# Weighting the early expert dot products while their gates are built, and prefetching the other gates

## The chip, the cores and the metric

One core of one Trainium2 chip runs the kernel. The metric is device time in microseconds (us) for one execution; the time before is the median of three runs. Engines are called PE (TensorE), DVE (VectorE), ACT (ScalarE), POOL (GpSimd) and SP (SyncE, which here only issues DMAs).

## The reference

The model is a decoder block on 512 tokens of width 1024. Two token mixers (a gated linear attention and a sparse latent attention) feed a residual stream; then a product-key expert layer (PEER) is applied, and this last layer is what the change touches:

```python
u = expert_u[ix]                       # ix: for each token, 8 heads x 16 experts of 16384
v = expert_v[ix]
a = gelu(einsum('td,thkd->thk', hx, u)) * gx     # gx: softmax weight of each picked expert
out = einsum('thk,thkd->td', a, v)
```

All arithmetic is float32.

## The kernel before, in words

The 512 tokens are two halves of 256. For the first half the expert layer is done by gathering: each picked expert's rows are fetched by an indirect DMA (POOL, L998), multiplied with the token on DVE (L1003) and added up on DVE (L1012). This `gather()` is a generator that runs in the background: `pump()` moves it on by a fixed share of a step wherever the other code calls it. `behind(i)` marks a DVE instruction after which the next gather instructions are to be issued.

For the second half (NDT = 256 tokens) the layer is done densely over all 16384 experts, in 128 chunks `ib` of 128 experts:

- `dots_of(ib)` loads two chunks of u (tile `up`, 1 MB, every second call), multiplies one chunk with the 256 tokens (`projT`, L184, one PSUM bank `pmm` of two) and writes Gelu of the result with ACT (L936) into a tile `a` of 128 x 256. Forty-eight such tiles (AHEAD = 48) can be held.
- `build_g(Tt)` builds the gate of every expert for every token, which is zero nearly everywhere. For 16 tokens at a time (a gate tile `gs` of 128 x 128 x 16, two buffers; 16 such tiles, eight for each of the token tiles Tt = 2 and 3), in two blocks of 8 tokens: DVE makes two comparison masks `pm` (L884) and `eq` (L887), ACT scales one into `qm` (L893), PE multiplies them (L898, in PSUM banks `psc` and `ptr`), ACT copies the result into `gs` (L899). Then ACT copies the gates of chunks 0 to 7 into two tiles `first_g` (L903), and SP writes the others, chunks 8 to 127, to a DRAM tensor `gd` (L904, 960 KB).
- `dense()` goes over the chunks: `weigh(ib + 5)` multiplies a dot product tile by its gate on DVE (L956); the gate of chunks from 8 on comes from `gd` in tiles `gtile` of eight chunks (L952, 1 MB, one buffer, asked for when the first of the eight is weighed). The weighted tile and the v chunk are each split into a high and a low part (L116 on ACT, L117 on DVE), and twelve matmuls (L186 to L188) add to four PSUM banks. Then one more dot product may be made, so that 80 of the 128 are made inside `dense()`.

Around it: dot products 0 to 7 are made before the experts of token tile 2 are picked, 8 to 23 before those of tile 3 are picked; `build_g(2)` is stepped between the parts of that second pick, and `build_g(3)` between dot products 24 to 47, one step (8 tokens) after each. Text order is a priority: a scheduler at compile time gives each engine a fixed order, in which an instruction goes ahead of earlier text if it is ready sooner by the scheduler's reckoning. On the chip each engine, and SP's queue of DMAs, then keeps its order. The tiles of `dense()` (pool `dn`) take over the memory of the tiles of `build_g` (pool `gb`), and each waits until the tile that lay there is free.

Of the kernel before, what the change touches and what calls it, by code (L numbers as in the profile page):

```python
# [59 lines left out]
def hybrid_block_kernel(ctx, tc, x, c_col, w_ada, b_ada, b_col, g1_col, g2_col, wT, wN, wM, w_br, w_o,  # L60
# [33 lines left out]
        nc.gpsimd.tensor_tensor(dst, dst, mhalf[:, :w], op=ALU.pow)  # L94

    x2d = [dr.tile([P, D], F32, name=f"x2d{i}") for i in range(NT)]
    gd = dr.tile([P // 8, P, NDT // GB, 8, GB], F32, name="gd")
    kvd = [dr.tile([2, P, TH], F32, name=f"kvd{i}") for i in range(8)]
    gated = [dr.tile([P, D], F32, name=f"gated{i}") for i in range(2)]

# [775 lines left out]
    def build_g(Tt):  # L876

        TB = 8
        for tb in range((Tt - NG) * P // GB, (Tt - NG + 1) * P // GB):
            gs = gb.tile([P, P, GB], F32, name="gs", bufs=2)  # L880
            for b in range(0, GB, TB):
                t0 = tb * GB + b
                pm = gb.tile([P, TB, P], F32, name="pm", bufs=2)
                nc.vector.tensor_tensor(pm, iof[:, None, :].to_broadcast([P, TB, P]),  # L884
                                        i2T[:, t0:t0 + TB, None].to_broadcast([P, TB, P]), op=ALU.is_equal)
                e = gb.tile([P, TB // 2, P, 2], BF16, name="eq", bufs=2)
                pace[0] = nc.vector.tensor_tensor(  # L887
                    e, iob[:, None].to_broadcast([P, TB // 2, P, 2]),
                    i1T[:, t0:t0 + TB].rearrange("p (g t) -> p g t", t=2)[:, :, None, :].to_broadcast([P, TB // 2, P, 2]),
                    op=ALU.is_equal).ins  # L890
                qm = gb.tile([P, TB, P], F32, name="qm", bufs=2)
                for t in range(TB):
                    nc.scalar.activation(qm[:, t], e[:, t // 2, :, t % 2], AF.Copy, scale=gaT[:, t0 + t:t0 + t + 1])  # L893
                for t4_ in range(0, TB, 4):
                    turn[0] += 1
                    p = (psc, ptr)[turn[0] % 2]().rearrange("p (t i) -> p t i", t=4)
                    for t in range(4):
                        nc.tensor.matmul(p[:, t], pm[:, t4_ + t], qm[:, t4_ + t], start=True, stop=True)  # L898
                    nc.scalar.copy(gs[:, :, b + t4_:b + t4_ + 4], p.rearrange("p t i -> p i t"))  # L899
                pump()  # L900
                yield
            for q in range(2):
                nc.scalar.copy(first_g[q][:, tb], gs[:, 4 * q:4 * q + 4])  # L903
            nc.sync.dma_start(gd.rearrange("c p b i t -> b p c i t")[tb, :, 1:], gs.rearrange("p (c i) t -> p c i t", i=8)[:, 1:])  # L904


    def finish(Tt, x2, peer):
# [18 lines left out]
    def dots_of(ib):  # L926
# [5 lines left out]
            nc.sync.dma_start(up[0], u_t[ib // 2])  # L932
        p = pmm(True)
        projT(p[:, :NDT], [up[0][:, ib % 2]], h2[1])
        a = ap.tile([P, NDT], F32, name="a", bufs=AHEAD)
        nc.scalar.activation(a, p[:, :NDT], AF.Gelu)  # L936
        return a

    def dense(ahead):
        banks = [psc, psc, ptr, ptr]  # L940
        acc = [[banks[2 * i + n]() for n in range(2)] for i in range(NT - NG)]
        gt = [None]
        weighted = []

        def weigh(ib):

            if ib < 8:
                g = first_g[ib // 4][:, :, ib % 4]
            else:
                if ib % 8 == 0:  # L950
                    gt[0] = dn.tile([P, NDT // GB, 8, GB], F32, name="gtile", bufs=1)
                    nc.sync.dma_start(gt[0], gd[ib // 8])  # L952
                g = gt[0][:, :, ib % 8]
            a = ahead.pop(0)
            a3 = a.rearrange("p (b t) -> p b t", t=GB)
            behind(nc.vector.tensor_tensor(a3, a3, g, op=ALU.mult))  # L956
            weighted.append(a)

        made = [len(ahead)]
        for ib in range(LEAD):  # L960
            weigh(ib)
        late_ops = []
        vb = x2 = None
        for ib in range(P):
# [6 lines left out]
                    nc.sync.dma_start(x2[:, i], x2d[NG + i])  # L971
            if ib + LEAD < P:
                weigh(ib + LEAD)
            a = hp.tile([P, 2, NDT], F32R, name="as", tag="h" + "hl"[ib % 2])
            v = wp.tile([P, 2, D], F32R, name="vs", tag="w2", bufs=2)
            split(a[:, 0], a[:, 1], weighted.pop(0))
            split(v[:, 0], v[:, 1], vb[:, ib % 2])
            a, v = [[t[:, 0], t[:, 1]] for t in (a, v)]
            late_ops.append((ib, a, v))
# [8 lines left out]
                        mm(acc[i][n], [t[:, ts_] for t in a], [t[:, ns] for t in v], jb == 0, jb == P - 1)  # L988
            late_ops.clear()
            while made[0] < AHEAD + (ib + 1) * (P - AHEAD) // (P - 16) and made[0] < P:  # L990
                ahead.append(dots_of(made[0]))
                made[0] += 1
            pump()
        for i in range(NT - NG):
            finish(NG + i, x2[:, i], acc[i])
# [133 lines left out]
    nc.gpsimd.iota(iob, pattern=[[1, P], [0, 2]], base=0, channel_multiplier=0, allow_small_or_imprecise_dtypes=True)  # L1129
    iof = gb.tile([P, P], BF16, name="iof")  # L1130
    nc.gpsimd.iota(iof, pattern=[[1, P]], base=0, channel_multiplier=0, allow_small_or_imprecise_dtypes=True)
    ahead = []

    first_g = [wp.tile([P, NDT // GB, 4, GB], F32, name="first_g", tag="raw", bufs=NRAW) for _ in range(2)]
    building = iter(())
    background[:] = [[gat, RATE_G, 0.0]]
    for Tt in range(NG, NT):
        ahead += [dots_of(len(ahead) + i) for i in range(DOTS[Tt - NG])]
        for h0 in range(0, 8, HG):
            for _ in pick(Tt, h0):  # L1140
                next(building, None)
# [2 lines left out]
        picks_T(Tt)  # L1144
        drain(building)
        building = build_g(Tt)
    while len(ahead) < AHEAD:
        ahead.append(dots_of(len(ahead)))
        next(building, None)
    drain(building)  # L1150
    rest_eng.close()
# [2 lines left out]
    nc.sync.dma_start(fing, rowb(fin_g, D))  # L1154
    nc.sync.dma_start(gate2, gated[1])
    background[:] = [[gat, RATE_DENSE, 0.0]]
    dense(ahead)
    drain(gat)


# [65 lines left out]
```

## Time and profile before

| what | value |
|---|---|
| median of three runs | 1875.56 us (1866.99 to 1878.46) |
| profiled execution, whole | 1862.8 us |
| its span (first to last instruction) | 1860.9 us |
| PE busy | 1723.5 us (93%) |
| DVE busy | 1431.9 us (77%) |
| ACT busy | 722.9 us (39%) |
| moved by DMA | 583.81 MB, mean 314 GB/s |

All views below are of the one profiled execution. "Busy" of PE is modelled from pipelined matmuls. The granted clock is a share of full speed: 1.00 is 2.4 GHz, and the lower of the two levels is 1.2 GHz. The gates are built from about 1005 to 1157 us, the dense stage runs from about 1180 to 1849 us.

### The profile page before, as it was taken

How to read it: one execution, taken by the hardware profiler on the slowest of the kernel's cores; microseconds unless marked ns; L12 is line 12 of the kernel's file. 1: busy time of each engine (PE TensorE's matmuls, PEld its weight loads, DVE VectorE, ACT ScalarE, POOL GpSimd, SP SyncE). 2: the span in 40 equal slices, each digit the busy share in tenths (PEclk: the TensorE clock that was granted, in tenths of full speed). 3: DMA queues.
4: the chain of work that ended last, by engine and by line, in shares of the span. 5: the costliest groups of instructions: out<-in, count | busy, mean ns of one | idle time of the engine just before them, and what ended most of it. 6: DMA issues, size and time to landing. Idle time of an engine off the chain costs nothing.

```text
span 1860.9 us, 24908 instructions
## 1 busy us (share of the span) xinstructions
PE 1723.5 (93%) x8898; PEld 1462.8 (79%) x8898; DVE 1431.9 (77%) x2993; ACT 722.9 (39%) x1693; POOL 504.7 (27%) x459
## 2 busy tenths in 40 slices
PE   6999999989999988989999889898999999999995
PEld 3888999878766876877778778687778888887874
DVE  5798545339999778658997888778778887887886
ACT  3544465333121134002245767333334433433443
POOL 0012000001563556643441555111112121211120
PEclk8999999989998999989999999899999999999998
DMA  8757566625886899996776999999989999999992
GB/s 292 287 182 265 192 193 206 225 88 204 285 294 215 313 338 385 392 378 243 279 284 238 393 369 359 415 422 394 401 345 410 392 404 393 412 410 372 421 361 99
DMA packets 156238, 583.81 MB, mean 314 GB/s; under 512 B 14529, under 2 KB 51521, under 8 KB 121426
## 3 DMA queue, kind: packets, MB, share of 16 engines
q1 hardware_dynamic: 100818, 313.76, 45.4%
q0 software_dynamic: 55296, 268.46, 37.4%
q8 instruction: 70, 1.15, 0.2%
q14 instruction: 54, 0.44, 0.1%
HBM read 559.10 MB, written 23.07 MB: 313 GB/s over the span
## 4 chain that ended last, share of the span: by engine, by line
PE 52%; DVE 17%; issue 12%; DMA 12%; POOL 5%; ACT 2%; SPq 0%; POOLq 0%; DVEq 0%; ACTq 0%
PE pmm L184 19%; DMA grow<-rows,ids 6%; POOL grow L998 4%; DVE grow L1003 3%; PE pmx L184 3%; PE pmm L188 2%; PE pmm L187 2%; PE pmm L186 2%; PE psc L187 2%; PE psc L188 2%; DMA gd<-gs 2%; PE ptr L188 2%; PE ptr L187 2%; DMA gtile<-gd 2%; PE psc L186 2%
## 5 line engine op out<-in xcount | busy, mean ns | idle before, releaser
L998 POOL DMA_INDIRECT grow<-rows,ids x384 | 446.9, 1164 | 897.9 <-DVE h2n L1012 500.6
L184 PE MATMUL pmm<-h2h,up 128*128 128x256 f32 x2048 | 470.2, 381 | 4.4 <-ACT a L936 2.8
L184 PEld LDWEIGHTS pmm<-h2h,up 128*128 128x128 f32 x2048 | 384.8, 191 | 57.4 <-ACT a L936 3.6
L1003 DVE SCALAR_TENSOR_TENSOR grow<-grow,h2n 128x1024 f32<-128x1024 f32 x256 | 310.0, 1217 | 56.0 <-DMA grow<-rows,ids 55.6
L1012 DVE SCALAR_TENSOR_TENSOR gacc<-grow,dots,gacc 128x1024 f32<-128x1024 f32 x127 | 162.2, 1277 | 18.9 <-DMA grow<-rows,ids 18.2
L117 DVE TENSOR_TENSOR vs<-vb,vs 128x1024 fp32r<-128x1024 f32 x128 | 158.1, 1235 | 22.8 <-ACT vs L116 22.7
L1012 DVE SCALAR_TENSOR_TENSOR h2n<-grow,dots,h2n 128x1024 f32<-128x1024 f32 x127 | 162.3, 1278 | 0.0
L116 ACT CAST vs<-vb 128x1024 fp32r<-128x1024 f32 x128 | 133.3, 1042 | 0.0
L117 DVE TENSOR_TENSOR w<-raw,w 128x1024 fp32r<-128x1024 f32 x79 | 98.0, 1240 | 45.7 <-ACT w L116 45.3
L187 PE MATMUL psc<-vs,as 128*128 128x512 f32 x256 | 104.5, 408 | 26.5 <-DVE vs L117 26.5
L186 PE MATMUL psc<-vs,as 128*128 128x512 f32 x256 | 115.8, 459 | 6.4 <-ACT vs L116 6.4
L116 ACT CAST w<-raw 128x1024 fp32r<-128x1024 f32 x79 | 82.6, 1046 | 72.7 <-PE pmm L188 33.1
L936 ACT ACTIVATE a<-pmm 128x256 f32<-128x256 f32 x128 | 49.0, 383 | 149.0 <-PE pmm L184 148.7
L188 PE MATMUL psc<-vs,as 128*128 128x512 f32 x256 | 102.6, 401 | 0.0
L184 PE MATMUL pmm<-hh,raw 128*128 128x256 f32 x416 | 98.5, 384 | 3.8 <-DVE yp L687 1.9
L188 PE MATMUL ptr<-vs,as 128*128 128x512 f32 x256 | 101.9, 398 | 0.0
L187 PE MATMUL ptr<-vs,as 128*128 128x512 f32 x256 | 101.8, 398 | 0.0
L186 PE MATMUL ptr<-vs,as 128*128 128x512 f32 x256 | 100.3, 397 | 0.0
L116 ACT CAST as<-a 128x256 fp32r<-128x256 f32 x128 | 51.5, 402 | 121.7 <-PE ptr L188 118.9
L1051 ACT ACTIVATE dots<-dots 128x1 f32<-128x1 f32 x128 | 25.9, 202 | 173.9 <-DVE grow L1003 173.6
L94 POOL TENSOR_TENSOR rs<-rs,mhalf 128x1 f32<-128x1 f32 (+1 forms) x24 | 18.1, 755 | 266.3 <-DVE rs L93 266.2
L184 PEld LDWEIGHTS pmm<-hh,raw 128*128 128x128 f32 x416 | 77.0, 191 | 16.2 <-DVE yp L687 2.3
(375 smaller groups left out, 3521.5 us busy)
## 6 DMA issues: line engine op xcount, KB each, us to landing
up<-u_t SPq DMA_DIRECT2D x64, 1024.0 KB, 9.4
vb<-v_t SPq DMA_DIRECT2D x64, 1024.0 KB, 9.3
raw<-wT SPq DMA_DIRECT2D x74, 512.0 KB, 4.5
adaw<-w_ada SPq DMA_DIRECT2D x20, 1024.0 KB, 6.8
raw<-wN SPq DMA_DIRECT2D x32, 512.0 KB, 4.3
raw<-w_br SPq DMA_DIRECT2D x32, 512.0 KB, 4.6
raw<-w_pq SPq DMA_DIRECT2D x32, 512.0 KB, 4.3
gd<-gs SPq DMA_DIRECT2D x16, 960.0 KB, 10.0
```

What stands on the lines that cost most here:

```text
L94: nc.gpsimd.tensor_tensor(dst, dst, mhalf[:, :w], op=ALU.pow)
L116: (hi_eng or nc.scalar.copy)(hi, src)
L117: i = (eng or nc.vector).tensor_tensor(lo, src, hi.bitcast(F32), op=ALU.subtract)
L184: nc.tensor.matmul(dst, a[0], b[0], start=first, stop=last, **kw)
L186: nc.tensor.matmul(dst, a[0], b[0], start=first, stop=False, **kw)
L187: nc.tensor.matmul(dst, a[0], b[1], start=False, stop=False, **kw)
L188: nc.tensor.matmul(dst, a[1], b[0], start=False, stop=last, **kw)
L936: nc.scalar.activation(a, p[:, :NDT], AF.Gelu)
L998: nc.gpsimd.indirect_dma_start(out=dst, out_offset=None, in_=table, in_offset=bass.IndirectOffsetOnAxis(ap=index[0][:, r:r + 1], axis=0))
L1003: nc.vector.scalar_tensor_tensor(u, u, 1.0, h2n[i], op0=ALU.mult, op1=ALU.mult, accum_out=dots[i][:, r:r + 1])
L1012: nc.vector.scalar_tensor_tensor(gacc, v, w, gacc, op0=ALU.mult, op1=ALU.add)
L1051: nc.scalar.activation(w, w, AF.Gelu)
```

## The change

Four things are done:

1. The 48 tiles `a` become one tile `kept` of 48 rows x 256 tokens. While a gate tile is built, the dot products made so far in the text (`m` of them: 24 for the first eight gate tiles, 27 to 41 for the others) are multiplied by their gates on DVE, in one instruction. For the chunks up to 47 whose dot products come later in the text, ACT copies the gates into their rows of `kept`.
2. A dot product of chunk 24 to 47 then finds `d` of its 256 tokens with a gate already in its row. For these ACT writes Gelu to a small tile `dg` (two buffers), and DVE multiplies it onto the row; for the other tokens ACT writes Gelu to the row as before.
3. Gates of chunks 0 to 47 are no longer written to `gd` or read back: a write is 640 KB, and ten gate tiles are read instead of fifteen. `first_g` is gone, and `weigh` does nothing below chunk 48.
4. The ten are read with two buffers: chunks 48 to 55 are asked for at the start of `dense()`, ahead of its first v chunk, and each next eight when the eight before them begin to be weighed. The second buffer lies where half of the `as` tiles were; `as` becomes one tile with four parts in the other half.

```diff
-    gd = dr.tile([P // 8, P, NDT // GB, 8, GB], F32, name="gd")
+    gd = dr.tile([(P - AHEAD) // 8, P, NDT // GB, 8, GB], F32, name="gd")
...
-            for q in range(2):
-                nc.scalar.copy(first_g[q][:, tb], gs[:, 4 * q:4 * q + 4])
-            nc.sync.dma_start(gd.rearrange("c p b i t -> b p c i t")[tb, :, 1:], gs.rearrange("p (c i) t -> p c i t", i=8)[:, 1:])
+            m, ts_ = made[0], slice(tb * GB, (tb + 1) * GB)
+            if m:
+                behind(nc.vector.tensor_tensor(kept[:, :m, ts_], kept[:, :m, ts_], gs[:, :m], op=ALU.mult))
+            if m < AHEAD:
+                nc.scalar.copy(kept[:, m:, ts_], gs[:, m:AHEAD])
+            built[0] = (tb + 1) * GB
+            nc.sync.dma_start(gd.rearrange("c p b i t -> b p c i t")[tb], gs.rearrange("p (c i) t -> p c i t", i=8)[:, AHEAD // 8:])
...
-        a = ap.tile([P, NDT], F32, name="a", bufs=AHEAD)
-        nc.scalar.activation(a, p[:, :NDT], AF.Gelu)
-        return a
-
-    def dense(ahead):
+        a = kept[:, ib % AHEAD]
+        d = built[0] if ib < AHEAD else 0
+        if d < NDT:
+            nc.scalar.activation(a[:, d:], p[:, d:NDT], AF.Gelu)
+        if d:
+            t = gb.tile([P, NDT], F32, name="dg", bufs=2)[:, :d]
+            nc.scalar.activation(t, p[:, :d], AF.Gelu)
+            behind(nc.vector.tensor_tensor(a[:, :d], a[:, :d], t, op=ALU.mult))
+        made[0] += 1
+
+    def dense():
...
+        as4 = hp.tile([P, 4, 2, NDT], F32R, name="as", tag="hh")
+        gts = []
+
+        def load_g(c):
+
+            if c < P // 8:
+                pool, tag = ((dn, "gtile"), (hp, "hl"))[c % 2]
+                gts.append(pool.tile([P, NDT // GB, 8, GB], F32, name="gtile", tag=tag))
+                nc.sync.dma_start(gts[-1], gd[c - AHEAD // 8])
+
+        load_g(AHEAD // 8)
 
         def weigh(ib):
 
-            if ib < 8:
-                g = first_g[ib // 4][:, :, ib % 4]
-            else:
-                if ib % 8 == 0:
-                    gt[0] = dn.tile([P, NDT // GB, 8, GB], F32, name="gtile", bufs=1)
-                    nc.sync.dma_start(gt[0], gd[ib // 8])
-                g = gt[0][:, :, ib % 8]
-            a = ahead.pop(0)
-            a3 = a.rearrange("p (b t) -> p b t", t=GB)
-            behind(nc.vector.tensor_tensor(a3, a3, g, op=ALU.mult))
-            weighted.append(a)
-
-        made = [len(ahead)]
-        for ib in range(LEAD):
-            weigh(ib)
+            if ib < AHEAD:
+                return
+            if ib % 8 == 0:
+                load_g(ib // 8 + 1)
+            a3 = kept[:, ib % AHEAD].rearrange("p (b t) -> p b t", t=GB)
+            behind(nc.vector.tensor_tensor(a3, a3, gts[ib // 8 - AHEAD // 8][:, :, ib % 8], op=ALU.mult))
+
...
-            a = hp.tile([P, 2, NDT], F32R, name="as", tag="h" + "hl"[ib % 2])
+            a = as4[:, ib % 4]
             v = wp.tile([P, 2, D], F32R, name="vs", tag="w2", bufs=2)
-            split(a[:, 0], a[:, 1], weighted.pop(0))
+            split(a[:, 0], a[:, 1], kept[:, ib % AHEAD])
...
+    kept = ap.tile([P, AHEAD, NDT], F32, name="kept")
+    made, built = [0], [0]
```

## Rows read from the trace of the kernel before

**Rows 1.** The page: engine, busy us, share of the span, instructions.
```profile
PE 1723.5 (93%) x8898; PEld 1462.8 (79%) x8898; DVE 1431.9 (77%) x2993; ACT 722.9 (39%) x1693; POOL 504.7 (27%) x459
...
DMA packets 156238, 583.81 MB, mean 314 GB/s; under 512 B 14529, under 2 KB 51521, under 8 KB 121426
```
**Rows 2.** Stretches: length, busy of PE, PEld, DVE, ACT, POOL, clock, DMA.
```profile
1005.00:1073.00 68.00, 62.53 (x393) 56.93 (x392) 56.35 (x53) 55.02 (x169) 35.05 (x25) 0.95 0.98 347
1073.00:1157.00 84.00, 74.06 (x435) 67.31 (x434) 68.48 (x66) 61.30 (x189) 45.87 (x33) 0.94 1.02 362
1157.00:1190.00 33.00, 24.95 (x100) 20.57 (x100) 19.47 (x33) 8.94 (x24) 6.12 (x5) 0.84 1.03 415
1190.00:1400.00 210.00, 198.23 (x867) 166.14 (x866) 168.90 (x254) 75.61 (x176) 37.36 (x38) 0.98 0.97 393
1400.00:1797.00 397.00, 394.60 (x1777) 334.79 (x1775) 326.61 (x447) 159.20 (x368) 80.00 (x80) 1.00 0.98 398
```
**Rows 3.** Waits from 1190 to 1797 us: total, times, longest.
```profile
DVE a L956 <- DMA gtile<-gd: 41.8, 11, 6.8
...
PE psc L187 <- DVE vs L117: 14.2, 7, 4.1
```
**Rows 4.** Waits from 1005 to 1157 us.
```profile
DVE pm L884 <- PE ptr L898: 29.5, 9, 11.3
ACT gs L899 <- DMA gd<-gs: 20.4, 5, 5.1
...
PE psc L898 <- ACT qm L893: 15.3, 5, 4.4
```
**Rows 5.** Timeline between build and dense stage: start, us, engine, idle before.
```profile
1156.39 17.00 PE L184 MATMUL pmm<-h2h,up 128*128 128x256 f32 x78
...
1163.80 0.74 SPq L967 DMA_DIRECT2D vb<-v_t  x1
...
1172.12 0.43 SPq L952 DMA_DIRECT2D gtile<-gd  x1
...
1179.83 0.80 PE L186 MATMUL psc<-vs,as 128*128 128x512 f32 x1 [6.44 <-ACT vs L116]
```
**Rows 6.** DMA issues of the whole span: times, KB each, median us to landing.
```profile
gd<-gs SPq DMA_DIRECT2D x16, 960.0 KB, 10.0
gtile<-gd SPq DMA_DIRECT2D x15, 1024.0 KB, 11.6
```
**Rows 7.** Groups of instructions from 1005 to 1157 us: busy, mean ns, idle before.
```profile
L998 POOL DMA_INDIRECT grow<-rows,ids x58 | 80.9, 1395 | 94.7 <-DVE gacc L1012 85.6 <-issue 8.2 <-DMA grow<-rows,ids 0.9
L184 PE MATMUL pmm<-h2h,up 128*128 128x256 f32 x311 | 80.9, 389 | 0.0
L1012 DVE SCALAR_TENSOR_TENSOR gacc<-grow,dots,gacc 128x1024 f32<-128x1024 f32 x60 | 76.7, 1279 | 2.9 <-DMA grow<-rows,ids 2.6
...
L936 ACT ACTIVATE a<-pmm 128x256 f32<-128x256 f32 x20 | 7.7, 387 | 3.1 <-PE pmm L184 3.1
L903 ACT COPY first_g<-gs 128x64 f32<-128x64 f32 x30 | 5.9, 246 | 0.3
```
**Rows 8.** Groups of instructions from 1190 to 1797 us.
```profile
L117 DVE TENSOR_TENSOR vs<-vb,vs 128x1024 fp32r<-128x1024 f32 x113 | 139.6, 1235 | 20.3 <-ACT vs L116 20.2
...
L956 DVE TENSOR_TENSOR a<-a,gtile 128x256 f32<-128x256 f32 x120 | 47.4, 420 | 41.8 <-DMA gtile<-gd 41.8
```
**Rows 9.** Timeline of PE as the building begins.
```profile
980.81 24.44 PE L184 MATMUL pmm<-h2h,up 128*128 128x256 f32 x112 [2.24 <-ACT a L936]
1005.09 1.05 PE L898 MATMUL psc<-qm,pm 128*128 128x128 f32 x8
1005.98 1.06 PE L898 MATMUL ptr<-qm,pm 128*128 128x128 f32 x8
```
**Rows 10.** The tiles of Gelu, from 900 to 1005 us, then to 1157 us.
```profile
L936 ACT ACTIVATE a<-pmm x23: 363/384/389, 916.9 to 1001.8; 128x256 f32<-128x256 f32 x23
...
L936 ACT ACTIVATE a<-pmm x20: 376/389/402, 1005.3 to 1155.9; 128x256 f32<-128x256 f32 x20
```

More of the change, by code (lines that the diff above doesn't have):

```diff
@@ L934, in dots_of @@
         projT(p[:, :NDT], [up[0][:, ib % 2]], h2[1])
-        a = ap.tile([P, NDT], F32, name="a", bufs=AHEAD)
-        nc.scalar.activation(a, p[:, :NDT], AF.Gelu)
-        return a
-    def dense(ahead):
+        a = kept[:, ib % AHEAD]
[8 more added lines that the diff above has]
+    def dense():
         banks = [psc, psc, ptr, ptr]
         acc = [[banks[2 * i + n]() for n in range(2)] for i in range(NT - NG)]
-        gt = [None]
-        weighted = []
-        def weigh(ib):
-            if ib < 8:
-                g = first_g[ib // 4][:, :, ib % 4]
-            else:
-                if ib % 8 == 0:
-                    gt[0] = dn.tile([P, NDT // GB, 8, GB], F32, name="gtile", bufs=1)
-                    nc.sync.dma_start(gt[0], gd[ib // 8])
-                g = gt[0][:, :, ib % 8]
-            a = ahead.pop(0)
-            a3 = a.rearrange("p (b t) -> p b t", t=GB)
-            behind(nc.vector.tensor_tensor(a3, a3, g, op=ALU.mult))
-            weighted.append(a)
-        made = [len(ahead)]
-        for ib in range(LEAD):
-            weigh(ib)
+        as4 = hp.tile([P, 4, 2, NDT], F32R, name="as", tag="hh")
[6 more added lines that the diff above has]
+        load_g(AHEAD // 8)
+        def weigh(ib):
+            if ib < AHEAD:
[4 more added lines that the diff above has]
+            behind(nc.vector.tensor_tensor(a3, a3, gts[ib // 8 - AHEAD // 8][:, :, ib % 8], op=ALU.mult))
         late_ops = []
@@ L990, in dense @@
             while made[0] < AHEAD + (ib + 1) * (P - AHEAD) // (P - 16) and made[0] < P:
-                ahead.append(dots_of(made[0]))
-                made[0] += 1
+                dots_of(made[0])
             pump()
@@ L1131, in hybrid_block_kernel @@
     nc.gpsimd.iota(iof, pattern=[[1, P]], base=0, channel_multiplier=0, allow_small_or_imprecise_dtypes=True)
-    ahead = []
-    first_g = [wp.tile([P, NDT // GB, 4, GB], F32, name="first_g", tag="raw", bufs=NRAW) for _ in range(2)]
+    kept = ap.tile([P, AHEAD, NDT], F32, name="kept")
+    made, built = [0], [0]
     building = iter(())
@@ L1137, in hybrid_block_kernel @@
     for Tt in range(NG, NT):
-        ahead += [dots_of(len(ahead) + i) for i in range(DOTS[Tt - NG])]
+        for _ in range(DOTS[Tt - NG]):
+            dots_of(made[0])
         for h0 in range(0, 8, HG):
@@ L1146, in hybrid_block_kernel @@
         building = build_g(Tt)
-    while len(ahead) < AHEAD:
-        ahead.append(dots_of(len(ahead)))
+    while made[0] < AHEAD:
+        dots_of(made[0])
         next(building, None)
@@ L1156, in hybrid_block_kernel @@
     background[:] = [[gat, RATE_DENSE, 0.0]]
-    dense(ahead)
+    dense()
     drain(gat)
```

## Prediction

> **What bounds the kernel now.** The page comes first: PE is busy 93% of the span, DVE 77%, ACT 39% [rows 1]. A kernel like that can gain only where PE stands or runs at a low clock, so the second view is the table of stretches, where each line gives length, busy PE and granted clock [rows 2]. From 1400 us to 1797 us PE is busy 394.6 of 397 us at clock 1.00: nothing to win but 2.4 us. The losses lie in four other stretches: 5.5 us idle at clock 0.95 in the first half of the gate building (1005 to 1073), 9.9 us at 0.94 in the second half (1073 to 1157), 8.1 us at 0.84 in the passage to the dense stage (1157 to 1190), 11.8 us at 0.98 in its first third (1190 to 1400).
>
> The third view is the waits, which say who is late. In the dense stage DVE stands 41.8 us in 11 waits for `gtile`, and PE stands 14.2 us for the low half of v that DVE makes [rows 3]. So a weigh that waits for its gates holds up the split that stands behind it on DVE. In the building ACT stands 20.4 us for the write of `gd` (its `gs` buffer isn't free), and PE 15.3 us for ACT's `qm` [rows 4]. In the passage PE finishes its dot products at 1173.4 and begins the dense stage at 1179.8 after 6.4 us [rows 5].
>
> **Dense stage: what is removed.** With chunks up to 47 weighted beforehand, the five gate tiles for chunks 8 to 47 vanish, and with them the early waits; each of the other ten is asked for eight chunks ahead, 43 us ahead by the 113 v splits in 607 us [rows 8], where a load takes 11.6 us to land [rows 6]. I take all gate waits of DVE away. PE's 14.2 us of standing go [rows 3], and with no pause the clock should stay up: 0.02 of 210 us is 4.2 us [rows 2]. Upper bound 18.4 us. Next late is DMA, which is busy 0.97 of that stretch at 393 GB/s [rows 2]. Four or five tiles less are 4 to 5 MB of 82.5 MB there (210 us x 393 GB/s); at the 415 GB/s seen in the passage the remaining 78 MB need 188 us, so 22 us could be taken out before DMA is the limit. Lower bound 6 us, if waits for u and v chunks take half and more of the place. I take 17. The 48 multiplies of 420 ns that leave the dense stage [rows 8], 20.2 us of DVE, count nothing of their own: DVE has 70 us idle in the 397 us where PE is full [rows 2].
>
> **Building: the write.** A `gd` write shrinks from 960 to 640 KB. It took 10.0 us to land in the median [rows 6], and the second half makes a gate tile every 84/8 = 10.5 us [rows 2], so half the writes are near or over what two buffers hide. At two thirds of the size, 6.7 us, most are hidden. I take 15 of ACT's 20.4 us away; since the waits of PE for `qm` total 15.3 [rows 4], this is worth 0 to 15 us, and some of the clock (0.05 x 68 + 0.06 x 84 = 8.4 us, [rows 2]).
>
> **Building: the added work.** No multiply over a strided row of several chunks is in the trace; its price comes from two DVE forms with two SBUF inputs, 420 ns for 256 elements and 1235 ns for 1024 [rows 8]: 148 ns fixed and 1.06 ns an element. Eight multiplies of 24 x 16 elements cost 0.556 us each, 4.4 us. The eight later ones have 27, 29, ... 41 rows, 4352 elements in all: 8 x 0.148 + 4.6 = 5.8 us. The 24 multiplies by `dg` have 128 (3 times), 144 to 240 (twice each) and 256 (7 times), 4864 elements: 3.6 + 5.2 = 8.7 us. Sum 18.9 us, 4.4 in the first half and 14.5 in the second, where DVE has 11.7 and 15.5 us idle [rows 2]. So it fits, but barely, and only if DVE can use its idle time, most of which (29.5 us, part of it from before 1005) is spent standing for a free `pm` [rows 4]. ACT: 246 ns for 64 elements and 387 for 256 [rows 7] give 199 ns fixed and 0.73 an element. It loses 32 copies (7.9 us), gains 16 copies of 384 down to 112 elements (3.8 + 2.9) and 17 second Gelus (3.4): 2.2 us more, against 15 us of waits saved.
>
> **Building: the filler that is lost.** This is the edit's hidden cost. PE runs dot products between the gate matmuls when it has nothing else: 23 Gelus were done by 1005 and 43 by 1157 [rows 10], so chunks 24 to 31 ran while `build_g(2)` was still at work. After the change a dot product from 24 on is finished only by a multiply with gates of tokens 0 to 127, which exist when that whole building is done. Two fill the `dg` buffers, two more the PSUM banks, then PE has no dot product to run; behind the third Gelu on ACT would stand the next `qm`. So four of the eight move later: 4 x 3.49 = 14 us (24.44 us for 7, [rows 9]). What this costs I work out from PE's own sum. Gate matmuls come 8 records in 0.89 us [rows 9], 512 records: 57 us. Dot products from 1005 to the passage: 311 + 78 records [rows 7, 5] at 16 each, 24.3, are 85 us. If the first half takes 57 us (its 68 less 11 of the 20.4 us that ACT waited for writes), PE fills 28.5 + 14 of it, and the other 28.5 + 71 us follow at full use: 1005 + 57 + 99.5 = 1161.5 in place of 1173.4. The gain in the building is thus about 12 us with no new waits, and below nothing (12 us lost) if the second half keeps its length and the 14 us of dot products and some pauses come on top.
>
> **The passage.** SP's queue gets a new item ahead of the first v chunk: the gates of chunks 48 to 55, which can't be read until the last `gd` write has landed. Before, the first v chunk was issued at 1163.8 and the first `gtile` at 1172.1 [rows 5], so every v chunk behind it may come up to 8.3 us later. In its favour, the gates are ready earlier than PE's last dot products, whose later place covers the wait: I count 0, with 8 us lost if that cover is gone and 8 us won (the 6.4 and some clock) if everything lands in time. Memory moves too: `dg` shifts the tiles of `gb`, so `dn` tiles wait on other ones; this lies within the same 8 us.
>
> For building and passage together, bounds are 25 us won and 20 us lost; nearest to the sum of PE is 12 won, and I take 7, since waits among three engines with two buffers always leave gaps.
>
> A row on POOL belongs here: its gather issue takes 1395 ns in the building, and it is busy 80.9 and idle 71 of 152 us, mostly for DVE's `gacc` [rows 7]. The Trainium skill, "SBUF — State Buffer", section "Summary: rules for kernel authors", says that when DVE reads two SBUF inputs while GpSimd reads SBUF, the one that issues second stands until the first is done. That speaks against moving multiplies into this stage. Whether it holds here the rows can't tell, since they don't split POOL's 1395 ns by what DVE did. By the rule, with the gather setting the end, the 18.9 us of multiplies come back as rival 4 has it; without, POOL's idle 71 us take them and the sum stays.
>
> **The sum.** 17 + 7 = 24 us. The profiled execution took 1862.8 us, 1860.9 of it span, 0.7% under the median of 1875.6; from it 1839, from the median 1852. The runs shown span 11.5 us, and about 1% (18.8 us) is what a measurement of this kernel tells from no change.
>
> **Rivals.**
> 1. The building gives back what the dense stage wins. For it: the lost filler (14 us), and DVE's 14.5 us in a half with 15.5 idle. Against it: PE's sum, which only moves. Dense 17 won, building 14 lost: 1872.
> 2. Slower. The multiply of each of the last eight gate tiles needs Gelu of the last of its `m` dot products. DVE keeps its order, so `pm` and `eq` of the next block stand behind it, ACT's `qm` behind these, and PE's gate matmuls behind that. It decides once fewer than `m` dot products are done when a gate tile ends. Before, 43 stood against 41 at the last one [rows 10]; with four moved later the margin is gone. Price: up to one dot product and Gelu, 3.9 us, eight times, 31 us, and the 14.5 us of DVE with it, less the 11 won by the smaller writes; less 17: 1893. Against it: the scheduler can put the needed dot product first.
> 3. DMA is the limit in the dense stage, and waits for u and v take the place of those for `gtile`. For it: share 0.97 to 1.03 [rows 2]. Against it: 1400 to 1797 is full at 398 GB/s. Dense 6 and building 4 won: 1866.
> 4. The gather sets the pace: DVE's 18.9 us push the 60 `gacc` steps (76.7 us, [rows 7]) back and the passage waits for them. 17 won, 19 lost: 1878. Against it: POOL's 71 us idle.
> 5. The scheduler's order undoes the plan, say by placing the multiplies late: no change, 1876.
>
> **How the numbers follow.** Forecast (both stages win) 0.64, with a range of its own from 1836 to 1866; rivals 0.16, 0.10, 0.06, 0.02 and 0.02. The range 1832 to 1880 takes in the bounds of the forecast and rivals 1, 3, 4 and 5, and leaves out rival 2 and a little below. Seven tenths of the forecast lie under 1857 (faster by over 1%): 0.46 with a trace of the others. Slower by over 1% is rival 2 with the worst of 4: 0.11. The rest, 0.43, is within 1%.
>
> **What would show it.** In the new profile: no wait of DVE for `gtile`, PE full from the passage on at clock 1.00; waits of ACT for `gd` near 5 us; PE with pauses of 10 to 15 us in the first half of the building and none in the second; dense start 5 to 12 us earlier. I am wrong if PE's idle time in the building grows by more than 10 us, if the first v chunk lands after the dot products end, or if DVE shows long waits for Gelu.

## The result, and the profile after

The changed kernel takes 1857.11 us in the median of six runs (1854.75 to 1866.37), the kernel before 1872.38 us (1866.38 to 1878.46) in the six runs beside it: a ratio of 0.9935, 95% interval 0.9911 to 0.9959. By the ratio it is faster by some 12 us (the two medians are 15.3 us apart). That is inside the 1% which the prediction called "no change", on the forecast side of zero, and half of the 23.6 us forecast. The profiled execution took 1861.09 us, its span 1859.4: one of the slower of its six, while the profiled execution of before (1862.8) lies below all six of before. So stages are compared here, not the two spans. The zero is the first copy of gates into `gs` (L899), since what lies ahead of it is unchanged and yet ends anywhere from 1001.5 to 1013.3 us in the fourteen profiles of this document.

| from the profiles, us | before | after | difference |
|---|---|---|---|
| first to last copy into `gs` (building) | 150.4 | 153.4 | +3.0 |
| first copy to the end of the last early dot product | 167.2 | 177.9 | +10.7 |
| PE then stands | 6.44 | 14.53 | +8.1 |
| so: first copy to the first dense matmul | 173.65 | 192.45 | +18.8 |
| first to last dense matmul | 668.9 | 644.45 | -24.4 |

The dense stage won more than forecast, and what stands ahead of it lost where a gain was forecast. The stretches of after, with columns as in [rows 2]; the third one is longer by 10 us, since the dense stage begins at 1203:

```profile
1005.00:1073.00 68.00, 53.01 (x310) 48.39 (x308) 54.54 (x56) 48.56 (x139) 35.71 (x24) 0.87 0.84 293
1073.00:1157.00 84.00, 77.03 (x456) 69.94 (x457) 80.49 (x94) 65.72 (x202) 57.20 (x34) 0.94 0.99 347
1157.00:1200.00 43.00, 31.43 (x157) 27.41 (x155) 12.68 (x25) 11.69 (x37) 2.40 (x2) 0.91 0.59 217
1200.00:1400.00 200.00, 197.01 (x873) 166.75 (x874) 164.94 (x225) 77.38 (x183) 49.71 (x41) 0.98 0.99 406
1400.00:1797.00 397.00, 397.00 (x1791) 337.64 (x1789) 327.84 (x449) 154.04 (x370) 95.83 (x81) 1.00 0.98 399
```

PE's idle time after 1200 is gone (the 3 us there lie before 1203); in its place PE stands 15 us in the first half of the building, where it stood 5.5 [rows 2], at a clock of 0.87 in place of 0.95, and 11.6 us in the passage. DVE is busy 80.5 of 84 us in the second half, where it was 68.5.

Whole stages again, building from first to last copy and dense stage from first to last matmul; here the windows follow the stages of each kernel. Before, then after:

```profile
1006.18:1156.59 150.41, 135.00 (x814) 122.72 (x813) 124.83 (x118) 115.52 (x355) 80.92 (x58) 0.94 1.01 358
1179.83:1849.10 669.27, 642.79 (x2816) 537.87 (x2816) 547.75 (x771) 258.88 (x594) 125.61 (x125) 0.98 0.94 381
```
```profile
1010.50:1163.86 153.36, 131.40 (x778) 119.50 (x777) 139.58 (x153) 118.86 (x356) 95.31 (x60) 0.91 0.95 329
1202.95:1847.80 644.85, 634.40 (x2816) 534.12 (x2816) 533.33 (x727) 250.67 (x591) 152.94 (x125) 0.99 0.95 385
```

With the same 2816 matmuls, PE's idle time in the dense stage fell from 26.5 to 10.4 us and its busy time, at a clock of 0.99 in place of 0.98, by 8.4 us: that is the 24.4. No wait of DVE for `gtile` is left there, where [rows 3] has 41.8 us.

The waits in the building of after, 1005 to 1164 us (total, times, longest), beside [rows 4]:

```profile
PE psc L898 <- ACT qm L893: 19.3, 8, 4.8
ACT qm L893 <- DVE eq L887: 12.7, 12, 1.9
DVE pm L884 <- PE ptr L898: 11.9, 2, 11.3
...
DVE kept L905 <- ACT gs L899: 7.7, 5, 3.2
ACT gs L899 <- DMA gd<-gs: 7.1, 3, 3.8
```

Before, 1005 to 1157 us:

```profile
ACT qm L893 <- DVE eq L887: 2.1, 3, 1.5
```

Read them as a chain. ACT waits 13.3 us less for the write, as meant. But DVE, which stood 29.5 us for PE, now stands 11.9, most of it once, and ACT stands for DVE's `eq`, 12.7 us where it was 2.1. DVE also stands 7.7 us at the new multiply (L905) for ACT's last copy into `gs`, with the work behind it in its order. The wait has moved from the write to DVE, and PE's wait for `qm` grew from 15.3 to 19.3.

The passage, waits of SP's queue from 1150 to 1200 us, then the timeline of the same stretch, beside [rows 5]:

```profile
SPq L961 <- PE pmm L184: 14.8, 1, 14.8
...
SPq L961 <- DMA gd<-gs: 8.6, 1, 8.6
```
```profile
1163.66 24.77 PE L184 MATMUL pmm<-h2h,up 128*128 128x256 f32 x114
...
1164.47 0.36 SPq L909 DMA_DIRECT2D gd<-gs  x1
...
1188.46 0.33 SPq L961 DMA_DIRECT2D gtile<-gd  x1
1188.88 0.38 SPq L1165 DMA_DIRECT2D fing<-fin_g  x1
...
1189.86 0.57 SPq L961 DMA_DIRECT2D gtile<-gd  x1
1190.47 0.45 SPq L979 DMA_DIRECT2D vb<-v_t  x1
...
1202.95 1.22 PE L186 MATMUL psc<-vs,as 128*128 128x512 f32 x2 [14.53 <-ACT vs L116]
```

After the last write of `gd` (1164.47) SP issues nothing for 24 us. Two loads of gates stand in its queue, not one, and the first of them goes into the memory of `hl`. Of the ten it is the second in the text, chunks 56 to 63: it was hoisted ahead of everything, presumably because it is ready early by the scheduler's reckoning (no run shows that reckoning). On the chip it waits for the write, and then for the last early dot products, whose u chunk still lies in `hl`. Everything behind it waits too, the gates of chunks 48 to 55 and the first v chunk among it, which was issued at 1163.8 before and at 1190.5 now, when PE had already run dry.

### The profile page after: what moved, and what is told of

Read it like the earlier page. It is cut to its first block, busy times and chain, and to the rows that moved or that the text cites. A ratio compares the mean times of both kernels' runs of the same rounds, so it can differ in the third digit from the quotient of the medians.

```text
span 1859.4 us, 25034 instructions
## 1 busy us (share of the span) xinstructions
PE 1725.0 (93%) x8898; PEld 1466.6 (79%) x8898; DVE 1432.8 (77%) x2985; ACT 719.0 (39%) x1694; POOL 540.5 (29%) x459
## 4 chain that ended last, share of the span: by engine, by line
issue 33%; PE 29%; DVE 15%; POOL 12%; DMA 8%; ACT 2%; SPq 0%; POOLq 0%; DVEq 0%; another core or an unknown queue 0%; ACTq 0%
POOL grow L1009 11%; PE pmm L184 8%; DMA grow<-rows,ids 4%; DVE grow L1014 3%; PE pmx L184 2%; PE pmm L187 2%; PE pmm L186 2%; PE pmm L188 2%; DVE gacc L1023 2%; DMA gd<-gs 2%; PE psc L898 2%; PE ptr L898 1%; DMA adaw<-w_ada 1%; PE pmx L187 1%; PE pmx L186 1%
## 5 line engine op out<-in xcount | busy, mean ns | idle before, releaser
L1009 POOL DMA_INDIRECT grow<-rows,ids x384 | 482.9, 1258 | 838.8 <-DVE h2n L1023 451.0
L184 PE MATMUL pmm<-h2h,up 128*128 128x256 f32 x2048 | 468.4, 381 | 5.0 <-ACT kept L943 3.1
L184 PEld LDWEIGHTS pmm<-h2h,up 128*128 128x128 f32 x2048 | 385.5, 191 | 59.3 <-ACT kept L943 3.9
L186 PE MATMUL psc<-vs,as 128*128 128x512 f32 x256 | 114.6, 454 | 14.5 <-ACT vs L116 14.5
L187 PE MATMUL psc<-vs,as 128*128 128x512 f32 x256 | 102.7, 401 | 10.4 <-DVE vs L117 10.4
L116 ACT CAST w<-raw 128x1024 fp32r<-128x1024 f32 x79 | 82.6, 1046 | 72.9 <-PE pmm L188 32.8
L184 PE MATMUL pmm<-hh,raw 128*128 128x256 f32 x416 | 99.8, 388 | 4.3 <-DVE bsg L689 2.1
L116 ACT CAST as<-kept 128x256 fp32r<-128x256 f32 x128 | 51.3, 403 | 133.7 <-PE ptr L187 128.9
L188 PE MATMUL psc<-vs,as 128*128 128x512 f32 x256 | 101.0, 395 | 0.0
L184 PEld LDWEIGHTS pmm<-hh,raw 128*128 128x128 f32 x416 | 77.9, 193 | 17.3 <-DVE bsg L689 2.5
L117 DVE TENSOR_TENSOR as<-kept,as 128x256 fp32r<-128x256 f32 x128 | 53.4, 423 | 47.0 <-ACT as L116 46.9
```

Of the source, the lines that this page charges most:

```text
L116: (hi_eng or nc.scalar.copy)(hi, src)
L117: i = (eng or nc.vector).tensor_tensor(lo, src, hi.bitcast(F32), op=ALU.subtract)
L184: nc.tensor.matmul(dst, a[0], b[0], start=first, stop=last, **kw)
L186: nc.tensor.matmul(dst, a[0], b[0], start=first, stop=False, **kw)
L187: nc.tensor.matmul(dst, a[0], b[1], start=False, stop=False, **kw)
L188: nc.tensor.matmul(dst, a[1], b[0], start=False, stop=last, **kw)
```

## The experiments

Twelve kernels ran. "Building" is the time from the first to the last copy into `gs`, "dots end" and "first dense matmul" count from the first copy. The columns of times are each from one profile, in us; the ratio is from the timed runs. Added up, the stages give up to 10 us less gain than the ratio in most rows (in e1_pin and e3_prefetch_only 1 to 3 us more), since all are set against one profile of before, whose execution lies below the six timed beside after. So the columns tell where time went, and the ratio how much.

| kernel | building | dots end | PE stands | first dense matmul | dense stage | ratio to before, 95% interval |
|---|---|---|---|---|---|---|
| before | 150.4 | 167.2 | 6.4 | 173.7 | 668.9 | 1 |
| after | 153.4 | 177.9 | 14.5 | 192.5 | 644.5 | 0.9935 (0.9911 to 0.9959) |
| e1_pin | 152.6 | 177.1 | 5.0 | 182.2 | 668.3 | 1.0059 (1.0030 to 1.0089) |
| e2_dg5 | 151.5 | 166.2 | 14.5 | 180.6 | 642.4 | 0.9892 (0.9858 to 0.9926) |
| e3_prefetch_only | 151.0 | 167.8 | 7.9 | 175.7 | 674.1 | 1.0046 (1.0024 to 1.0067) |
| e4_weight_only | 151.0 | 175.6 | 5.4 | 181.0 | 664.1 | 0.9984 (0.9961 to 1.0006) |
| e5_pin7 | 153.6 | 178.2 | 5.0 | 183.2 | 646.9 | 0.9905 (0.9882 to 0.9929) |
| e6_pin7_dg5 | 149.1 | 163.7 | 7.0 | 170.7 | 645.4 | 0.9831 (0.9804 to 0.9859) |
| e7_prefetch_only2 | 153.8 | 170.6 | 9.4 | 180.0 | 653.7 | 0.9917 (0.9888 to 0.9946) |
| e8_write960 | 157.7 | 182.2 | 14.4 | 196.6 | 643.8 | 0.9985 (0.9968 to 1.0002) |
| e9_nomult | 145.8 | 160.0 | 5.7 | 165.7 | 646.9 | 0.9808 (0.9778 to 0.9838) |
| e10_late6 | 150.0 | 164.6 | 5.0 | 169.6 | 646.7 | 0.9853 (0.9820 to 0.9885) |
| e11_gather80 | 133.9 | 157.6 | 1.4 | 159.0 | 667.5 | 0.9862 (0.9828 to 0.9895) |
| e12_gather60 | 129.0 | 156.5 | 1.4 | 158.0 | 696.7 | 1.0024 (1.0003 to 1.0045) |

**The passage: e1_pin, e5_pin7.** First theory: the hoisted load holds SP's queue. e1_pin keeps every load of gates behind the latest load of v.

```diff
-                nc.sync.dma_start(gts[-1], gd[c - AHEAD // 8])
+                with tc.issue_after(vload[0]) if vload[0] else ExitStack():
+                    nc.sync.dma_start(gts[-1], gd[c - AHEAD // 8])
...
-                nc.sync.dma_start(vb, v_t[ib // 2])
+                vload[0] = nc.sync.dma_start(vb, v_t[ib // 2]).ins
...
```

> The changed kernel with one edge more: each load of a gate tile is kept behind the latest v load of the text on SP's queue, so the tile of chunks 56 to 63 no longer stands first on that queue until the last dot product frees its buffer. Theory A (the queue's head holds up the v chunks): PE's 14.5 us of standing before its first dense matmul fall to 0 to 4 us, the dense stage starts 10 to 14 us earlier and the time falls to 1843 to 1847. Rival B (the passage is set by the last write of gates and by DMA): the first dense matmul moves by under 3 us and the time stays at 1854 to 1860.

PE stands 5.0 us in place of 14.5: that half holds. But the kernel got slower than before. Waits from 1200 to 1797 us:

```profile
DVE kept L974 <- DMA gtile<-gd: 34.0, 6, 9.1
```

Tied to the v load of its own step, each load of gates comes behind v loads that wait for their own buffers, so the eight chunks of lead are lost and all of the dense win with them (668.3 us). What hoists one load badly is what makes the other nine early. So e5_pin7 ties one load alone, that of chunks 56 to 63, behind the v load of chunks 4 and 5.

```diff
+                with tc.issue_after(vload[0]) if c == AHEAD // 8 + 1 else ExitStack():
+                    nc.sync.dma_start(gts[-1], gd[c - AHEAD // 8])
...
+                i = nc.sync.dma_start(vb, v_t[ib // 2])
+                if ib == 4:
+                    vload[0] = i.ins
...
```

> The changed kernel with one load moved: only the gate tile of chunks 56 to 63 is kept behind the v load of chunks 4 and 5 on SP's queue; all other gate loads stand where the changed kernel has them. e1_pin had kept every gate load behind the latest v load: its first dense matmul came 182 us after the building's first gate copy against 192, but DVE then stood 34 us for late gate tiles. If the queue's head was the passage's cost: first dense matmul 182 us after the first gate copy, no wait of DVE for gate tiles, time 8 to 11 us under the changed kernel (0.987 to 0.990 of the kernel before). If reading ahead costs DMA what it saves (rival), the dense stage is longer by the same 10 us and the time stays at 0.993.

The first dense matmul comes 9.2 us sooner, the dense stage keeps all but 2.4 us of its win, and the ratio is 0.9905, though its interval still overlaps that of after. SP's queue in e5_pin7, the first v chunk now 163.9 us after the first copy into `gs`, 180.0 in after:

```profile
1162.97 0.36 SPq L909 DMA_DIRECT2D gd<-gs  x1
1163.42 2.02 SPq L1169 DMA_DIRECT2D fing<-fin_g  x1
...
1172.32 0.32 SPq L963 DMA_DIRECT2D gtile<-gd  x1
1172.69 0.43 SPq L981 DMA_DIRECT2D vb<-v_t  x1
```

**The lost filler: e2_dg5, e6_pin7_dg5.** With `dg` in two buffers PE can run only a few dot products past those that wait for gates. e2_dg5 gives it five.

```diff
-            t = gb.tile([P, NDT], F32, name="dg", bufs=2)[:, :d]
+            t = gb.tile([P, NDT], F32, name="dg", bufs=5)[:, :d]
```

> The changed kernel with five dg buffers in place of two, so that seven in place of four dot products can run before the gates of tokens 0 to 127 are complete. If the lost filler is what lengthened the building: PE's standing from 1005 to 1073 us falls from 15 to 5 to 8 us, the last dot product ends 6 to 10 us earlier and, since the first dense load waits for it, the time falls to 1847 to 1852. If DVE's added work lengthened it: the building ends as late as before and the time stays within 3 us of 1857.

The dots end 11.7 us sooner than in after. The rows that show why count the records of dot products (L184) in the first 72.9 us after the first copy. Before, after, e2_dg5:

```profile
L184 PE MATMUL pmm<-h2h,up 128*128 128x256 f32 x152 | 39.9, 389 | 0.0
```
```profile
L184 PE MATMUL pmm<-h2h,up 128*128 128x256 f32 x64 | 17.1, 380 | 0.0
```
```profile
L184 PE MATMUL pmm<-h2h,up 128*128 128x256 f32 x112 | 28.9, 381 | 0.0
```

At 16 records each, 5.5 dot products had left that stretch, and three came back. e6_pin7_dg5 joins this with e5_pin7's edit.

> Both repairs: the load moved as in e5_pin7, and five dg buffers as in e2_dg5. The dot products should end 166 us after the first gate copy (e2_dg5), and v chunks come as soon as the last write of gates has landed: first dense matmul at 174 to 178 us against 180.6 in e2_dg5 and 192 in the changed kernel. Time 0.984 to 0.988 of the kernel before; if both repairs remove the same wait, no better than e2_dg5 (0.989).

It has the lowest ratio here of the kernels that compute the reference, 0.9831 (medians 1843.06 us beside 1872.02 of before). The two gains add: the first dense matmul comes 21.7 us sooner than in after, where the repairs alone brought 9.2 and 11.8.

**Halves of the change: e3_prefetch_only, e4_weight_only, e7_prefetch_only2, e8_write960.** e3_prefetch_only is the kernel before with two buffers for its fifteen gate tiles, each asked for eight chunks ahead and tied as in e1_pin (and with `as` as one tile, to make the room).

```diff
+                pool, tag = ((hp, "hl"), (dn, "gtile"))[c % 2]
+                gts.append(pool.tile([P, NDT // GB, 8, GB], F32, name="gtile", tag=tag))
+                with tc.issue_after(vload[0]) if vload[0] else ExitStack():
+                    nc.sync.dma_start(gts[-1], gd[c])
...
```

> The kernel before, with the gate tiles of chunks 8 to 127 read through two buffers eight chunks ahead (behind the v load, as in e1_pin) and as in one tile; nothing is weighted in the building and all fifteen tiles are read. If the gate waits alone are the loss of the dense stage: first to last dense matmul takes 669 - 14 to 18 us, the building is as before, the time falls to 1854 to 1860. If DMA is the limit there, PE waits for v or u instead and the time stays above 1864.

A miss with e1_pin's cause: DVE stands 44.4 us for `gtile`, as much as before, and the kernel is slower. It says nothing of prefetching as such. e7_prefetch_only2 therefore ties only the second load (`if c == 2`).

> As e3_prefetch_only (the kernel before with the gates read through two buffers eight chunks ahead, no weighting in the building), but only the first load into the second buffer is held behind a v load; the others stand where the scheduler puts them. If e3_prefetch_only lost because its loads were late in the queue: no wait of DVE for gate tiles, first to last dense matmul 645 to 655 us against 669, time 0.990 to 0.994. If fifteen tiles are too much for DMA in the dense stage whatever their order: PE waits stay at 10 us and more, time 0.997 to 1.003.

Now DVE stands 13.2 us for `gtile`, the dense stage is 15.2 us shorter than before, and the ratio 0.9917: two buffers alone, with one load put right, win as much as the whole change did. With the same repair the whole change (e5_pin7, 0.9905) can't be told from them; only with five `dg` buffers (e6_pin7_dg5) does weighting ahead pay, by an interval clear of both. e4_weight_only is the other half: after with one buffer, asked for when its first chunk is weighed, and `as` where it was.

```diff
-                pool, tag = ((dn, "gtile"), (hp, "hl"))[c % 2]
-                gts.append(pool.tile([P, NDT // GB, 8, GB], F32, name="gtile", tag=tag))
+                gts.append(dn.tile([P, NDT // GB, 8, GB], F32, name="gtile", bufs=1))
...
-                load_g(ib // 8 + 1)
+                load_g(ib // 8)
...
```

> The changed kernel without the reading ahead: one gate buffer, asked for when its first chunk is weighed, as in the kernel before; the weighting in the building stays. The second gate tile is no longer at the head of the queue, so the passage is short. Expected: building some 7 us longer than before, passage no longer than 5 us, the early gate waits gone and the late ones (16.8 us of DVE from 1400 us on) kept with 2 to 4 us of PE standing. Time 1850 to 1858; if the late waits cost more than they did, 1860 to 1866.

Weighting alone is no change (0.9984): the dense stage wins 4.8 us, since DVE stands no less for ten late loads than for fifteen (47.6 us, 41.8 before), and the stretch ahead of it loses 7.3. e8_write960 is after with the old size of the write.

```diff
-    gd = dr.tile([(P - AHEAD) // 8, P, NDT // GB, 8, GB], F32, name="gd")
+    gd = dr.tile([P // 8, P, NDT // GB, 8, GB], F32, name="gd")
...
+            nc.sync.dma_start(gd.rearrange("c p b i t -> b p c i t")[tb, :, 1:], gs.rearrange("p (c i) t -> p c i t", i=8)[:, 1:])
...
```

> The changed kernel with writes of 960 KB as before (chunks 8 to 47 are written and not read). Order of instructions on PE, DVE and ACT is that of the changed kernel. If the smaller write is worth what the prediction took (15 us of ACT's waits): ACT's waits for the write go from 7 back to 18 to 22 us, the building from 154 to 160 to 166 us, time 1862 to 1868, ratio 0.997 to 1.000. If the writes had been hidden behind DVE's and PE's work: ratio 0.993 to 0.995.

ACT's waits for the write go from 7.1 to 13.8 us (18 to 22 expected), the building from 153.4 to 157.7, and the ratio to 0.9985. So the smaller write is worth 4 us by the profiles and 9 by the ratios, whose two intervals leave 4 inside.

**What sets the building's pace: e9_nomult, e11_gather80, e12_gather60.** In every kernel so far the building takes 149 to 158 us, whatever ACT's wait for the write. e9_nomult is e6_pin7_dg5 without the multiply of L905, so its output is not weighted for those chunks.

```diff
-            if m:
-                behind(nc.vector.tensor_tensor(kept[:, :m, ts_], kept[:, :m, ts_], gs[:, :m], op=ALU.mult))
```

> This is the kernel of e6_pin7_dg5 without the 16 DVE multiplies of line 905; it leaves out the weighting of the dot products that were made before their gate tile, so those chunks go into the output unweighted. DVE loses about 11 us of work in the building (8 x 0.55 and 8 x 0.8 us). Theory 'DVE's added work has taken ACT's waits' place in the building': building, from the first gs copy to the last, falls from 149.1 us to 139 to 143, waits of ACT for eq (9.2 us) fall by half or more, first dense matmul 5 to 10 us sooner than 170.7 us after the first gs copy, ratio to before 0.977 to 0.980. Theory 'the building is paced by something else (gathers, PE or the write)': building 147 to 151 us, ratio 0.982 to 0.985 as e6.

Between the two theories: 10.2 us of DVE taken away give 3.3 us of building and 5.0 at the first dense matmul (profiles of e6_pin7_dg5 and e9_nomult). The halves say more. The first half, to the 32nd of the 64 copies, in before, after, e6_pin7_dg5 and e9_nomult:

```profile
1006.18:1072.32 66.14, 60.67 (x379) 55.22 (x378) 55.67 (x53) 53.95 (x166) 34.50 (x25) 0.95 1.00 354
```
```profile
1010.50:1082.62 72.12, 53.83 (x314) 49.26 (x312) 64.09 (x64) 54.22 (x156) 41.89 (x29) 0.83 0.89 302
```
```profile
1013.27:1082.32 69.05, 59.49 (x362) 53.26 (x360) 64.10 (x64) 55.11 (x163) 41.57 (x29) 0.95 0.92 331
```
```profile
1005.34:1066.41 61.07, 55.83 (x362) 50.17 (x360) 55.02 (x52) 54.13 (x163) 35.76 (x24) 1.00 0.92 333
```

The length follows DVE's busy time (third of the engines): 55.7 and 55.0 us in the short halves, 64.1 in the long ones. Of the 8.4 us added, seven multiplies are 3.9, and five more `gacc` steps of the gather (31 in place of 26) are 6.3; one `pm` less takes off 1.3. But DVE's work is not all: e6_pin7_dg5's first half is 3 us shorter than after's with 64.1 us in both. Without the multiplies five gathers leave the first half with them, and four come back in the second, which grows from 80.1 to 84.7 us. So DVE is shared between the gates, the multiplies and the gather. To test that without leaving anything out, e11_gather80 and e12_gather60, both on e6_pin7_dg5, move the gather on more slowly in the building and faster in the dense stage.

```diff
-RATE_ADA, RATE_GLA, RATE_DSA, RATE_G, RATE_DENSE = 0.4, 0.75, 0.9, 1.0, 1.05
+RATE_ADA, RATE_GLA, RATE_DSA, RATE_G, RATE_DENSE = 0.4, 0.75, 0.9, 0.8, 1.15
```

> This is e6_pin7_dg5 with the background gather moved on at a rate of 0.8 in place of 1.0 a step while the gates are built, and of 1.15 in place of 1.05 in the dense stage: about 12 of the 63 gacc steps of 1.28 us leave the building, some 15 us of DVE, and the output stays the reference's. Theory 'DVE, with the gathers and the added multiplies, sets the building's pace': building 138 to 144 us in place of 149.1, waits of ACT for eq under 5 us in place of 9.2, first dense matmul 5 to 9 us sooner than 170.7 us after the first gs copy, ratio to before 0.978 to 0.981, dense stage within 2 us of 645.4. Rival 'PE is the pace, with 136 of 149 us busy': building 147 us or more and ratio 0.982 to 0.986; if the later gathers hold up v's split in the dense stage, that stage grows by 5 us or more.

> This is e6_pin7_dg5 with the gather at 0.6 in place of 1.0 a step in the building and at 1.25 in place of 1.05 in the dense stage: about 25 gacc steps, 32 us of DVE, leave the building. If DVE sets the pace of the building until PE does, it gains little over the kernel with 0.8: building 134 to 142 us, PE busy over 95% of it, ratio 0.976 to 0.981 as long as the dense stage, where DVE stands 90 of 613 us, takes the steps; if not, the dense stage grows by 5 to 15 us and the ratio is 0.983 or more. Rival 'PE is the pace already': building 147 us or more.

The building in e6_pin7_dg5, e11_gather80 and e12_gather60, then its second half in e12_gather60:

```profile
1013.27:1162.38 149.11, 136.12 (x824) 122.43 (x823) 140.02 (x154) 119.17 (x358) 97.78 (x60) 0.97 0.96 342
```
```profile
1005.03:1138.88 133.85, 124.75 (x782) 113.20 (x781) 124.38 (x140) 116.88 (x356) 81.04 (x49) 0.97 0.93 324
```
```profile
1006.58:1135.53 128.95, 121.06 (x764) 109.39 (x763) 108.29 (x125) 115.67 (x353) 53.72 (x38) 0.99 0.88 298
```
```profile
1062.10:1135.53 73.43, 71.32 (x445) 64.59 (x444) 59.27 (x74) 62.64 (x196) 30.01 (x22) 1.00 0.95 327
```

The building of e11_gather80 is 133.9 us, 15.3 less than e6_pin7_dg5's, for some 15 us of `gacc`; in e12_gather60 129.0. So DVE's work is the main part of what set the building's length after the change. Three limits belong to that. Moving the gather also takes load off DMA and changes PE's order: ACT's waits for the write fell from 7.4 to 3.8 us, and some 40 records of dot products moved behind the building, so the dots end only 6.1 us sooner. The next 16 us taken off DVE gave 4.9; PE is nearly full in the second half by then, 71.3 of 73.4 us. And the kernel before had no more DVE work than e11_gather80 (124.8 and 124.4 us) in a building 16.5 us longer: there, with 20.4 us of ACT's waits for the write [rows 4], DVE was not the limit.

Nothing is won in all: the dense stage takes 22 and 51 us more. Waits there, 1175 to 1850 us, in e11_gather80:

```profile
DVE grow L1018 <- DMA grow<-rows,ids: 94.0, 70, 5.5
...
PE psc L187 <- DVE vs L117: 21.4, 20, 2.3
```

DVE now stands 94 us for gathered rows, 39.2 in e6_pin7_dg5, and v's split stands behind it in DVE's order. DVE's idle time in the dense stage was no room for the gather; why the rows come late there is open.

**What is left of the passage: e10_late6.** In e6_pin7_dg5 the gates of chunks 48 to 55 still go ahead of the first v chunk.

```diff
-                with tc.issue_after(vload[0]) if c == AHEAD // 8 + 1 else ExitStack():
+                with tc.issue_after(vload[0]) if c <= AHEAD // 8 + 1 else ExitStack():
...
-        load_g(AHEAD // 8)
...
                 if ib == 4:
                     vload[0] = i.ins
+                    load_g(AHEAD // 8)
```

> This is e6_pin7_dg5 with the gates of chunks 48 to 55 also kept on SP's queue behind the load of v chunks 4 and 5. Theory 'what is left of the passage is a v chunk behind the first gate tile': the standing of PE before the first dense matmul falls from 6.96 us to 3 to 5 us, ratio to before 0.980 to 0.982, with DVE standing for gtile under 2 us, since these gates are wanted some 200 us later. Theory 'the last write or the memory of the v tiles sets the first dense matmul': standing 6 to 8 us and ratio 0.982 to 0.985, as e6.

PE stands 5.0 in place of 7.0 us, the first dense matmul comes 1.1 us sooner, and the ratio of 0.9853 can't be told from e6_pin7_dg5's. SP waits 5.5 us for the last write to land before it issues the first v chunk, at 1165.5, ten us after that write: the write holds it, with or without gates ahead of it. The gates of chunks 48 to 55 are also wanted sooner than the expectation says: their first multiply starts at 1197.1, some 22 us after the first dense matmul.

## Why the prediction was half right, point by point

**Dense stage: mechanism right, size too small.** Forecast 17 of at most 18.4, measured 24.4. The upper bound was mis-sized, in its clock term above all: it took 14.2 us of PE's standing and 4.2 for the clock, the latter priced in the first third of the stage alone. Over the whole stage 16.0 us of standing and 8.4 of busy time came back, the granted clock going from 0.98 to 0.99. The DMA limit that pulled the term down (rival 3) didn't bite: 406 and 399 GB/s were moved with PE full. By e7_prefetch_only2 and e4_weight_only, the second buffer is worth 15.2 and the smaller number of tiles 4.8; the last 4 come with both.

**The write: right in size, half of it for the reason given.** 15 of 20.4 us of ACT's waits were to go, 13.3 went; but with the old size (e8_write960) 6.6 of these were gone too, so the smaller write itself took 6.7. It is worth 4 to 9 us, inside the 0 to 15.

**Prices of the added work: right.** 384 elements took 553 ns for the forecast 556. The sixteen multiplies came to 10.2 us, the 24 by `dg` to 8.7, as forecast. The longest row, 656 elements, took 843 ns by 148 + 1.06 x 656 = 843.

**"So it fits, but barely": wrong, the step that failed first.** The sum set 18.9 us of work against 27 us of idle DVE and counted it free. But DVE was late at the moments that count, not on the average: when it gives `eq` later, ACT makes `qm` later, and PE's gate matmul is later. That, with the five more gathers and 5.6 us that DVE stood at L905 for ACT's last copies, made the first half 6 us longer, where 11 us less were forecast. e9_nomult and e11_gather80 show DVE's part by taking work off it; how the 6 us divide among the three is open.

**"PE's own sum": wrong.** Four dot products were to move (5.5 did), and "PE fills" was to make it harmless: dots ending at 1161.5 in place of 1173.4. They ended 10.7 us later, counted from the first copy, near the step's own lower bound (12 lost). PE was not full in a first half that DVE paced (53.8 of 72.1 us), so a dot product that left it ran behind it, at its full 3.5 us; and the first half's clock fell to 0.83. Even with both cures (e6_pin7_dg5) the dots end only 3.5 us sooner than before.

**The passage: size right, cause wrong.** "8 lost if that cover is gone" is what was lost (8.1 us). But the item named, the gates of chunks 48 to 55, costs some 1 us (1.1 by the profile of e10_late6). The one that cost was not looked for: the load of the second buffer, which the text puts 200 us later and the scheduler puts first. The bounds for building and passage are uneven too: 12 and 8 us make the 20 lost, but not the 25 won, and no term of the sum gives the other 5.

**Rivals.** Rival 1, the building gives back the dense win, is what happened, with 18.8 us given back for 14 forecast; it gave 1872 only because the dense win was put at 17. Rival 2's waits for Gelu were 3.0 us, once, at the last gate tile, and 1.3 for `dg` up to there, not 31; DVE's 7.7 us at L905 for ACT's copies are the same mechanism at another input, which no rival names. Rival 4 had the right engine and the wrong end: the passage did not wait for the gather, the gates did.

POOL's gather issue went from 1395 to 1589 ns in the building. In its second half it took 1377 ns before, 1785 in e6_pin7_dg5 and 1629 in e9_nomult, without L905's multiplies, so these are the smaller part of the rise. DVE's own instructions kept their length (`gacc` 1279 and 1277 ns). The rule of the Trainium skill, "SBUF — State Buffer", section "Summary: rules for kernel authors", has the second of DVE and GpSimd to issue stand until the first is done, if DVE has two SBUF inputs and the GpSimd operation reads SBUF. The trace agrees in direction, for POOL alone; no run here shows a time that hangs on it.

**The forecast of 1852** had gains of 17 and 7. Measured, they are 24.4 won and 18.8 lost, which leaves 5.6 by the two profiles; the ratio of the timed runs has 12. That the time fell as forecast, and lies in the range, is in part luck: with 18.8 lost, the 17 of the dense stage would have been no gain, and the error of that term made up for the one in the building.

**The signs.** No wait of DVE for `gtile` and a full PE in the dense stage came as said; so did PE's 15 us of pauses in the first half, but the second half had 7 where none was forecast, and the dense stage began 18.8 us later, counted from the first copy, in place of 5 to 12 earlier. Of the three signs of being wrong one came: the first v chunk was issued at 1190.5, after the dots had ended at 1188.4. PE's idle time in the building grew by 6.6 us, under the 10, and no wait of DVE for Gelu was over 3.0 us.

## What to carry to other kernels

A load with a buffer of its own is not an early load. In a queue that keeps its order it is as late as the slowest thing ahead of it, and it makes all behind it as late as its own buffer (23.4 us here): before adding one, look up who holds that memory, and where the scheduler will put the load. Where work is moved onto an engine that feeds others step by step, its mean idle time is no cover. And filler that loses its input early is not moved for nothing: give it enough buffers to run ahead.

## What the runs showed that was not expected

A rate of the background gather that is 20% lower in one stage cost 22 us in the next (e11_gather80), with the same gather in sum: some twelve steps more made the dense stage that much longer, although DVE is idle for 111 of its 645 us in after.

The lower size of the write did not show in every landing. The chain of waits of after, in the first half of the building (start, us, what):

```profile
1027.35 0.59 ACT gs L899
...
1028.17 15.90 DMA gd<-gs
```

This write of 640 KB kept the next copy into `gs` waiting until 1044, where the median of 960 KB before was 10.0 us [rows 6] and the prediction took 6.7. Why is open: the profile of after has no landing times of these writes.

In the first half PE's clock fell to 0.83 where PE stood 18 of 72 us (after), and was 0.95 where it stood 5.5 of 66 (before).
